# A decoder layer on one core: 48 weight units loaded ahead, gathers in steps 7 to 116 with a step's lag, the last 24 units in two rings of buffers

## The chip, the core and the metric

The kernel runs on one core of a Trainium2 chip, in one launch. The metric is device time in microseconds. Its engines: TensorE (PE, matmuls; PEld is its loading of weights), VectorE (DVE), ScalarE (ACT), GpSimd (POOL) and SyncE (SP, which here only starts transfers). Each engine works through its own list of instructions in order; a list is fixed when the program is built, and semaphores make an instruction wait for others.

## What is computed

A layer over 256 tokens of width 2048: a projection, a pooling mixer beside sparse attention, an output projection and a layer norm, then a retrieval among 128 x 128 = 16384 experts, and a second norm. The change lies in the retrieval:

```python
v1, i1 = lax.top_k(s1, PEER_TOPK)            # 16 of 128 keys, twice
v2, i2 = lax.top_k(s2, PEER_TOPK)
best, pos = lax.top_k(cand, PEER_TOPK)       # 16 of the 256 pairs, for each of 8 heads
expert = jnp.take_along_axis(cidx, pos, axis=-1)
act = jax.nn.gelu(jnp.einsum('td,thkd->thk', xc, u[expert]), approximate=False)
out = jnp.einsum('thk,thkd->td', gate * act, v[expert])
```

Each token needs the products of its row with 128 chosen rows of u.

## The kernel before

Instead of gathering whole rows of u, the kernel multiplies the first 1408 of the 2048 columns densely, for all 16384 experts, and gathers only the last 640 columns. This is the u stage, and the change lies in it and in the stage ahead of it.

**The dense part** runs over 128 steps (`i2`). A step is 11 pieces of 128 columns, each multiplied in three matmuls (`mm3`: high and low halves of float32). The weights come in units of 512 columns by 128 partitions, four pieces each: 352 units, 2.75 in a step. A unit is loaded by SP (256 KB), split into `hi` (ACT, L95) and `lo` (DVE, L96; in the first 20 units every fourth on POOL) and multiplied. There are four `hi`/`lo` pairs, so splits run at most four units ahead of PE. At the end of a step ACT copies the sums into `S` (L687).

**Where units wait.** `S` fills up step by step, and its parts that are not yet written serve as buffers: a planner (L520 to L532) gives unit n a place in `S`, and `load_ahead` (L534) loads it when unit m is split. `PRE` sets how many loads go out in the stage before, while the last 12 column tiles of the query projection `w_q` (48 units, in a ring of four `raw` buffers) are worked on. `PRE = (1, 2)` is one in two, thus 24. The last 24 units (`RAW_END`) find no place in `S` and pass through the four `raw` buffers.

**The gathered part** is 256 gathers, one for each slot and half of the tokens: POOL starts a transfer of 128 rows of 640 numbers (L666), and DVE multiplies it with the tokens' columns and sums (L691, called a product below). `spread` deals them out over the steps `G0` to `GE`, here 12 to 124, each gather and its product in one step. Their buffers are a ring of three (`gath`) and, two times in five (`GR = 2`), the ring of four `raw`, which the last 24 units share. Indices (`e_idx`) come from the top-16 search, head by head, mostly on DVE.

The order of each engine's list is set by a scheduler from program order and priorities; loads and splits of units have a high priority (`AHEAD`). After the u stage come the extraction (32 blocks of 8 tokens; `at`, `bt` and `a_hot` on DVE and POOL, loads `bc` in the ring `gath`, products `junk` L733) and the v stage, which is built like the u stage. The change leaves the lists of the v stage as they were, and those of the extraction but for its first blocks.

Of the kernel before, what the change touches and what calls it, by code (L numbers as in the profile page):

```python
# [9 lines left out]
F32 = mybir.dt.float32  # L10
# [8 lines left out]
P = 128  # L19
# [12 lines left out]
GU = D - KDU * P  # L32
# [6 lines left out]
UNIT = 512  # L39
EB = 8  # L40
GB = 3
GR = 2
GR_END = 128
RB = 4
RAW_END = 24
FIRST = 2
# [4 lines left out]
IDLE = 28  # L51
EARLY0 = 16
EARLY_N = 2
PRE = (1, 2)
BP = 3
AHEAD = 3000
G0 = 12
GE = 125
LEAD = 5
LAG = 1  # L60
KEEP0 = 40
# [11 lines left out]
def layer(ctx, tc, A, out):  # L73
    nc = tc.nc
# [10 lines left out]
    def bankA(name):  # L85
        return psA.tile([P, 512], F32, name=name, tag="a")
# [4 lines left out]
    last_split, last_copy, last_load, last_moment = [None], [None], [None], [None]  # L91
    after_unit = [None]

    def split(hi, lo, src, eng=None):
        last_copy[0] = nc.scalar.copy(hi, src).ins  # L95
        last_split[0] = (eng or nc.vector).tensor_tensor(lo, src, hi.bitcast(F32), op=ALU.subtract).ins  # L96

    def raw_unit():
        return stream.tile([P, UNIT], F32, name="raw", bufs=RB)

    def load_unit(src, raw=None, eng=None):
        with tc.high_priority(offset=AHEAD):
            if raw is None:
                raw = raw_unit()
                last_load[0] = nc.sync.dma_start(raw, src).ins
            pair = tuple(stream.tile([P, UNIT], F32R, name=s, bufs=4) for s in ("hi", "lo"))
            split(pair[0], pair[1], raw, eng)
        return pair
# [10 lines left out]
    def mm3(o, l, r, first, last):  # L119
        mm(o, l[0], r[0], start=first, stop=False)  # L120
        mm(o, l[0], r[1], start=False, stop=False)  # L121
        return mm(o, l[1], r[0], start=False, stop=last).ins  # L122
# [9 lines left out]
    gath = ctx.enter_context(tc.tile_pool(name="gath", bufs=1))  # L132
# [370 lines left out]
    def step_of(i2, sl=slice(0, T)):  # L503
        return S[:, i2 // 2, sl.start // 2:sl.stop // 2, i2 % 2, :]
# [4 lines left out]
    def s_part(p):  # L509
        return S[:, p].rearrange("p a b c -> p (a b c)")  # L510

    def paired(a):
        return a.rearrange("p (t j) -> p t j", j=2)
# [5 lines left out]
    U_UNITS = P * KDU // 4  # L519
    place, follow, free, n = {}, {}, set(range(1, P // 2)), 0  # L520
    for m in range(-WQ_UNITS, U_UNITS):
# [3 lines left out]
        n = max(n, m + 1)  # L525
        for _ in range((m * PRE[0] % PRE[1] < PRE[0]) if m < 0 else 2):
            fit = [p for p in free if 2 * p > (4 * n + 3) // KDU + 1]
# [6 lines left out]
    def load_ahead(m):  # L534
        for n in follow[m]:
            p = place[n]
            with tc.issue_after(last_load[0]):
                last_load[0] = nc.sync.dma_start(s_part(p), A["u_d"][n]).ins

    count = [-WQ_UNITS]  # L540
# [117 lines left out]
    gorder = [(tt, h * PK + k) for h in range(HEADS) for k in range(PK) for tt in range(NT)]  # L658

    def gather(table, tt, slot, n):  # L660
        if table is A["u_g"] and slot < GR_END and count[0] % (GB + GR) >= GB:
            g = stream.tile([P, n], F32, name="g", tag="raw", bufs=RB)
        else:
            g = gath.tile([P, n], F32, name="g", bufs=GB)
        count[0] += 1
        nc.gpsimd.indirect_dma_start(out=g, out_offset=None, in_=table,  # L666
                                     in_offset=bass.IndirectOffsetOnAxis(ap=e_idx[:, tt, slot:slot + 1], axis=0))
        return g

    def spread(i, i0, i1):  # L670
        n = i1 - i0
        return gorder[len(gorder) * min(max(i - i0, 0), n) // n:len(gorder) * min(max(i - i0 + 1, 0), n) // n]

    after_unit[0] = None
    count[0] = 0
    w = None
    for i2 in range(P):
        ps = bankA("ups")[:, :T]
        for kt in range(KDU):
            un, k = divmod(i2 * KDU + kt, 4)  # L680
            if k == 0:
                p = place.get(un)
                w = load_unit(A["u_d"][un], None if p is None else s_part(p),
                              nc.gpsimd if un < POOL_UE and un % 4 in POOL_UU else None)
                load_ahead(un)
            mm3(ps, tuple(a[:, k * P:(k + 1) * P] for a in w), hs[kt], kt == 0, kt == KDU - 1)
        nc.scalar.copy(step_of(i2), paired(ps))  # L687
        with tc.issue_after(last_split[0]):
            for tt, slot in spread(i2, G0, GE):
                g = gather(A["u_g"], tt, slot, GU)  # L690
                nc.vector.scalar_tensor_tensor(g, g, 1.0, h_gath[:, tt], op0=ALU.mult, op1=ALU.mult,  # L691
                                               accum_out=pd[:, tt, slot:slot + 1])

# [92 lines left out]
    for m in range(P * NC):  # L786
        v_follow[m] = []
        i2, c = divmod(m, NC)
# [9 lines left out]
    def v_unit(i2, c):  # L798

        m = i2 * NC + c  # L800
        for n in v_follow[m]:
            with tc.high_priority(offset=AHEAD), tc.issue_after(last_load[0]):
                last_load[0] = nc.sync.dma_start(s_part(v_place[n]), A["v_d"][n]).ins
        return s_part(v_place[m]) if m in v_place else None
# [38 lines left out]
    for i2 in range(P - GL):  # L843
        wt = weights(i2, tokens if i2 == 0 else [slice(0, T)])
        units = []
        for c in range(NC):
            raw = v_unit(i2, c)
# [113 lines left out]
```

## Time and profile before

| | us |
|---|---|
| three runs | 1741.22, 1744.06, 1749.92 (median 1744.06) |
| the profiled execution | 1744.31 |
| its span, from the first instruction to the last | 1742.5 |
| PE busy / DVE busy / ACT busy / POOL busy | 1667.0 / 1433.3 / 899.2 / 872.9 |
| u stage: copy of step 0 to copy of step 127 | 492.20 to 1006.72 |

The profile is of one execution; durations below come from it. An engine's busy time in a stretch is shown beside the stretch's length; "PEclk" is the granted clock of TensorE as a share of its full speed. A matmul's record is longer than the distance between two, since they are pipelined: it is the distance that counts.

### The profile page before, as it was taken

The page shows a single profiled execution, that of the slowest core. Times are in us where ns is not written, and L with a number is a line of the kernel's source. Part 1 is how long each engine was busy: PE and PEld are TensorE (multiplying, and loading weights), DVE is VectorE, ACT ScalarE, POOL GpSimd, SP SyncE. Part 2 cuts the span into 40 slices and gives each one's busy share as a digit, 9 for nine tenths or more (in the row PEclk, how much of TensorE's full clock was granted, in tenths as well). Part 3 has the DMA queues.
Part 4 walks back from the last instruction along what each step waited for, and adds up shares of the span by engine and source line. Part 5 has one row for each costly group of instructions (what it writes and reads, how often), then busy time and mean ns, then how long its engine had stood idle before and what let it go on. Part 6 is the DMA issues. An engine that isn't in the chain of part 4 may idle for free. (4 is left out here: it accounts for less than half of the span.)

```text
span 1742.5 us, 33159 instructions
## 1 busy us (share of the span) xinstructions
PE 1667.0 (96%) x10680; PEld 1487.2 (85%) x10680; DVE 1433.3 (82%) x3486; ACT 899.2 (52%) x1917; POOL 872.9 (50%) x892
## 2 busy tenths in 40 slices
PE   8999999999899999999999889988999999999996
PEld 8999888889889999999999788876787888888883
DVE  6766677679999989888888798876778888889896
ACT  6545565444445555555554357764454555555551
POOL 0000000026886666566665588857647644556562
PEclk9999999999999999999999999999999999999998
DMA  7667667826688999999999932138999999999962
GB/s 219 177 188 193 198 184 253 258 93 218 217 288 290 343 352 337 318 338 353 340 334 321 306 107 59 52 104 287 303 327 327 381 334 331 340 314 329 354 199 89
DMA packets 206014, 451.13 MB, mean 259 GB/s; under 512 B 26928, under 2 KB 31472, under 8 KB 205328
## 3 DMA queue, kind: packets, MB, share of 16 engines
q1 hardware_dynamic: 164816, 297.93, 52.4%
q0 software_dynamic: 41024, 151.09, 25.0%
q8 instruction: 84, 1.38, 0.3%
q14 instruction: 90, 0.74, 0.1%
HBM read 444.59 MB, written 4.26 MB: 258 GB/s over the span
## 5 line engine op out<-in xcount | busy, mean ns | idle before, releaser
L95 ACT CAST hi<-S 128x512 fp32r<-128x512 f32 x677 | 420.0, 621 | 430.2 <-PE vacc L122 220.0
L96 DVE TENSOR_TENSOR lo<-S,hi 128x512 fp32r<-128x512 f32 x672 | 463.0, 698 | 95.8 <-ACT hi L95 88.0
L122 PE MATMUL ups<-hTh,lo 128*128 128x256 f32 x1408 | 391.8, 282 | 8.2 <-DVE lo L96 8.1
L120 PE MATMUL ups<-hTh,hi 128*128 128x256 f32 x1408 | 393.2, 281 | 4.4 <-ACT hi L95 4.2
L121 PE MATMUL ups<-hTl,hi 128*128 128x256 f32 x1408 | 392.8, 280 | 0.0
L666 POOL DMA_INDIRECT g<-u_g,e_idx x256 | 286.3, 1118 | 172.3 <-DVE g L691 121.2
L95 ACT CAST hi<-raw 128x512 fp32r<-128x512 f32 x327 | 201.3, 620 | 209.4 <-PE projT L121 58.9
L96 DVE TENSOR_TENSOR lo<-raw,hi 128x512 fp32r<-128x512 f32 x303 | 215.7, 716 | 111.8 <-ACT hi L95 110.0
L121 PE MATMUL vacc<-lo,wt 128*128 128x512 f32 x744 | 278.7, 401 | 6.9 <-DVE lo L96 6.8
L122 PE MATMUL vacc<-hi,wt 128*128 128x512 f32 x744 | 275.9, 398 | 0.0
L122 PEld LDWEIGHTS ups<-hTh,lo 128*128 128x128 f32 x1408 | 263.7, 189 | 13.0 <-DVE lo L96 12.1
L120 PEld LDWEIGHTS ups<-hTh,hi 128*128 128x128 f32 x1408 | 266.1, 189 | 5.9 <-ACT hi L95 5.9
L121 PEld LDWEIGHTS ups<-hTl,hi 128*128 128x128 f32 x1408 | 266.1, 189 | 0.0
L120 PE MATMUL vacc<-hi,wt 128*128 128x512 f32 x744 | 232.4, 401 | 7.5 <-ACT wt L95 6.9
L812 POOL DMA_INDIRECT g<-v_g,e_idx x139 | 161.7, 1163 | 130.7 <-DVE accg L820 107.6
L691 DVE SCALAR_TENSOR_TENSOR g<-g,h_gath 128x640 f32<-128x640 f32 x256 | 205.1, 821 | 14.7 <-DMA g<-u_g,e_idx 14.4
L812 POOL DMA_INDIRECT raw<-v_g,e_idx x117 | 138.0, 1179 | 85.3 <-DVE accg L820 67.0
L121 PEld LDWEIGHTS vacc<-lo,wt 128*128 128x128 f32 x744 | 141.2, 190 | 43.9 <-DVE lo L96 9.2
L120 PEld LDWEIGHTS vacc<-hi,wt 128*128 128x128 f32 x744 | 141.6, 191 | 42.9 <-ACT wt L95 7.5
L122 PEld LDWEIGHTS vacc<-hi,wt 128*128 128x128 f32 x744 | 141.2, 190 | 33.9 <-issue 0.5
L721 POOL TENSOR_SCALAR bt<-cst,slotT 128x128 f32<-128x128 f32 x192 | 125.5, 671 | 27.3 <-POOL bt L721 15.9
L295 POOL TENSOR_TENSOR bias<-bias,score 128x128 f32<-128x128 f32 (+1 forms) x16 | 11.3, 731 | 234.1 <-DMA bias<-relb 110.9
(241 smaller groups left out, 3067.4 us busy)
## 6 DMA issues: line engine op xcount, KB each, us to landing
S<-v_d SPq DMA_DIRECT2D x361, 256.0 KB, 5.1
S<-u_d SPq DMA_DIRECT2D x328, 256.0 KB, 5.4
raw<-w_t SPq DMA_DIRECT2D x100, 256.0 KB, 2.9
raw<-w_n SPq DMA_DIRECT2D x64, 256.0 KB, 2.9
raw<-w_o SPq DMA_DIRECT2D x64, 256.0 KB, 3.5
raw<-w_q SPq DMA_DIRECT2D x48, 256.0 KB, 3.2
bc<-i_dram SPq DMA_DIRECT2D x32, 256.0 KB, 3.3
raw<-u_d SPq DMA_DIRECT2D x24, 256.0 KB, 4.9
```

Of the source, the lines that this page charges most:

```text
L95: last_copy[0] = nc.scalar.copy(hi, src).ins
L96: last_split[0] = (eng or nc.vector).tensor_tensor(lo, src, hi.bitcast(F32), op=ALU.subtract).ins
L120: mm(o, l[0], r[0], start=first, stop=False)
L121: mm(o, l[0], r[1], start=False, stop=False)
L122: return mm(o, l[1], r[0], start=False, stop=last).ins
L295: nc.gpsimd.tensor_tensor(bias[:, tt, :n], bias[:, tt, :n], sel[:, tt, :n], op=ALU.add)
L666: nc.gpsimd.indirect_dma_start(out=g, out_offset=None, in_=table, in_offset=bass.IndirectOffsetOnAxis(ap=e_idx[:, tt, slot:slot + 1], axis=0))
L691: nc.vector.scalar_tensor_tensor(g, g, 1.0, h_gath[:, tt], op0=ALU.mult, op1=ALU.mult, accum_out=pd[:, tt, slot:slot + 1])
L721: eng.tensor_scalar(bt[j][:, i], iota, i2T[:, t:t + 1], None, op0=ALU.is_equal)
L812: nc.gpsimd.indirect_dma_start(out=g, out_offset=None, in_=A["v_g"], in_offset=bass.IndirectOffsetOnAxis(ap=e_idx[:, tt, slot:slot + 1], a ...
```

## The change

Five edits, all in or ahead of the u stage:

- `PRE` becomes (1, 1): 48 loads of u units, not 24, go out among the 48 loads of `w_q`.
- Gathers are dealt out over steps 7 to 116 (110 steps) rather than 12 to 124 (113 steps).
- A gather's product comes one step after the gather (`fetched`, `due`).
- Until slot 116 gathers use the `raw` ring four times in seven, so both rings whole; the last 24 gathers two times in five.
- The last 24 units pass through both rings, three of seven through `gath` and four through `raw`.

```diff
-GR = 2
-GR_END = 128
+GR = (4, 2)
+GR_END = 116
-PRE = (1, 2)
+PRE = (1, 1)
-G0 = 12
-GE = 125
+G0 = 7
+GE = 117
...
-        if table is A["u_g"] and slot < GR_END and count[0] % (GB + GR) >= GB:
+        if count[0] % (GB + GR[slot >= GR_END]) >= GB:
...
-                w = load_unit(A["u_d"][un], None if p is None else s_part(p),
+                raw = None if p is None else s_part(p)
+                if un >= U_UNITS - RAW_END and un % (GB + RB) < GB:
+                    raw = gath.tile([P, UNIT], F32, name="g", bufs=GB)
+                    with tc.high_priority(offset=AHEAD):
+                        last_load[0] = nc.sync.dma_start(raw, A["u_d"][un]).ins
+                w = load_unit(A["u_d"][un], raw,
...
-            for tt, slot in spread(i2, G0, GE):
-                g = gather(A["u_g"], tt, slot, GU)
+            due, fetched = fetched, [(tt, slot, gather(A["u_g"], tt, slot, GU)) for tt, slot in spread(i2, G0, GE)]
+            for tt, slot, g in due:
```

What this does to the engines' lists, at three places. First DVE where the units change from `S` to the raw buffers (units 327 to 332), before. A row `lo<-S` or `lo<-raw` is the split of one unit, a row `g,pd<-g,h_gath` one product; the numbers tell tiles apart and grow in program order:

```order
L96 TENSOR_TENSOR lo_13140<-S_4968,hi_13139 128x512
L96 TENSOR_TENSOR lo_13166<-raw_13163,hi_13165 128x512
L96 TENSOR_TENSOR lo_13184<-raw_13181,hi_13183 128x512
L691 SCALAR_TENSOR_TENSOR g_13203,pd_6643<-g_13203,h_gath_75 128x640
L691 SCALAR_TENSOR_TENSOR g_12764,pd_6643<-g_12764,h_gath_75 128x640
L96 TENSOR_TENSOR lo_13210<-raw_13207,hi_13209 128x512
L691 SCALAR_TENSOR_TENSOR g_12815,pd_6643<-g_12815,h_gath_75 128x640
L691 SCALAR_TENSOR_TENSOR g_12818,pd_6643<-g_12818,h_gath_75 128x640
L96 TENSOR_TENSOR lo_13228<-raw_13225,hi_13227 128x512
L96 TENSOR_TENSOR lo_13246<-raw_13243,hi_13245 128x512
```

And the same place now, from the split of unit 327, over unit 328, to the last product of all, behind which stands the split of unit 329 (`lo_13226`):

```order
L96 TENSOR_TENSOR lo_13188<-S_4968,hi_13187 128x512
L697 SCALAR_TENSOR_TENSOR g_12981,pd_6667<-g_12981,h_gath_75 128x640
L697 SCALAR_TENSOR_TENSOR g_12763,pd_6667<-g_12763,h_gath_75 128x640
...
L697 SCALAR_TENSOR_TENSOR g_13090,pd_6667<-g_13090,h_gath_75 128x640
L96 TENSOR_TENSOR lo_13208<-raw_13205,hi_13207 128x512
L697 SCALAR_TENSOR_TENSOR g_12924,pd_6667<-g_12924,h_gath_75 128x640
L697 SCALAR_TENSOR_TENSOR g_12926,pd_6667<-g_12926,h_gath_75 128x640
L697 SCALAR_TENSOR_TENSOR g_12983,pd_6667<-g_12983,h_gath_75 128x640
L697 SCALAR_TENSOR_TENSOR g_13033,pd_6667<-g_13033,h_gath_75 128x640
L697 SCALAR_TENSOR_TENSOR g_13035,pd_6667<-g_13035,h_gath_75 128x640
L697 SCALAR_TENSOR_TENSOR g_13092,pd_6667<-g_13092,h_gath_75 128x640
L704 CAST iota_e_13659<-cst_295 128x256
L96 TENSOR_TENSOR lo_13226<-g_13223,hi_13225 128x512
```

Before, 231 products stand ahead of the split of unit 327 and the other 25 among those of units 328 to 351. Now 222 stand ahead of unit 312's split (before 215), 244 ahead of unit 327's, six between units 327 and 328, six between 328 and 329, and none behind.

Second, the end of POOL's gathers in the changed kernel, in the order in which they are started:

```order
L666 DMA g_12763<-u_g,e_idx_72 128x640
L666 DMA g_12811<-u_g,e_idx_72 128x640
L666 DMA g_12870<-u_g,e_idx_72 128x640
L666 DMA g_13088<-u_g,e_idx_72 128x640
L666 DMA g_13090<-u_g,e_idx_72 128x640
L666 DMA g_12924<-u_g,e_idx_72 128x640
L666 DMA g_12926<-u_g,e_idx_72 128x640
L666 DMA g_12983<-u_g,e_idx_72 128x640
L666 DMA g_13033<-u_g,e_idx_72 128x640
L666 DMA g_13035<-u_g,e_idx_72 128x640
L666 DMA g_13092<-u_g,e_idx_72 128x640
```

Of these, 13088 and 13090 lie in the `raw` ring; the other nine follow each other through the three buffers of `gath`, and the next three tiles in that ring are the units 329 to 331.

Third, where the products begin on DVE, behind the last indices. Before:

```order
L627 CAST i1b_6608<-i12_74 128x256
L96 TENSOR_TENSOR lo_7358<-S_4968,hi_7357 128x512
L691 SCALAR_TENSOR_TENSOR g_7313,pd_6643<-g_7313,h_gath_75 128x640
L691 SCALAR_TENSOR_TENSOR g_7316,pd_6643<-g_7316,h_gath_75 128x640
L691 SCALAR_TENSOR_TENSOR g_7368,pd_6643<-g_7368,h_gath_75 128x640
L691 SCALAR_TENSOR_TENSOR g_7371,pd_6643<-g_7371,h_gath_75 128x640
L96 TENSOR_TENSOR lo_7382<-S_4968,hi_7381 128x512
```

And now:

```order
L627 CAST i1b_6632<-i12_74 128x256
L96 TENSOR_TENSOR lo_7384<-S_4968,hi_7383 128x512
L697 SCALAR_TENSOR_TENSOR g_7063,pd_6667<-g_7063,h_gath_75 128x640
L697 SCALAR_TENSOR_TENSOR g_7065,pd_6667<-g_7065,h_gath_75 128x640
L697 SCALAR_TENSOR_TENSOR g_7117,pd_6667<-g_7117,h_gath_75 128x640
L697 SCALAR_TENSOR_TENSOR g_7119,pd_6667<-g_7119,h_gath_75 128x640
L697 SCALAR_TENSOR_TENSOR g_7173,pd_6667<-g_7173,h_gath_75 128x640
L697 SCALAR_TENSOR_TENSOR g_7175,pd_6667<-g_7175,h_gath_75 128x640
L697 SCALAR_TENSOR_TENSOR g_7229,pd_6667<-g_7229,h_gath_75 128x640
L96 TENSOR_TENSOR lo_7411<-S_4968,hi_7410 128x512
```

The products begin at the same place of the list, some 35 units in, with seven in a row where four stood; by unit 56 there are 22 where there were 18.

## Rows read from the trace of the kernel before

**Rows 1.** Stretches of the span: length, busy us of each engine, clock, transfers.
```profile
395.00:475.00 80.00, 74.28 (x603) 72.34 (x602) 75.13 (x301) 31.39 (x73) 62.94 (x72) 0.98 0.70 221
475.00:550.00 75.00, 70.35 (x573) 67.44 (x571) 71.96 (x241) 36.79 (x84) 55.30 (x65) 1.00 0.87 285
550.00:575.00 25.00, 24.33 (x205) 23.92 (x205) 23.02 (x50) 12.11 (x24) 17.12 (x17) 1.00 0.90 298
575.00:947.70 372.70, 372.43 (x3193) 372.23 (x3192) 326.52 (x679) 193.92 (x361) 231.59 (x206) 1.00 0.96 341
947.70:1006.70 59.00, 50.01 (x363) 46.36 (x361) 44.76 (x99) 21.23 (x41) 32.39 (x32) 0.94 0.89 291
```

**Rows 2.** Timeline of ACT, copies of steps 16, 116 and 127: start, duration.
```profile
562.02 0.39 ACT L687 COPY S<-ups 128x256 f32<-128x256 f32 x1
...
947.66 0.39 ACT L687 COPY S<-ups 128x256 f32<-128x256 f32 x1 [2.67 <-PE ups L122]
...
1006.72 0.40 ACT L687 COPY S<-ups 128x256 f32<-128x256 f32 x1 [1.99 <-PE ups L122]
```

**Rows 3.** Waits from 947.7 to 1006.7: who for whom, total, times, longest.
```profile
ACT hi L95 <- DMA raw<-u_d: 18.8, 12, 3.6
POOL g L666 <- DVE g L691: 16.7, 11, 3.5
...
DVE g L691 <- DMA g<-u_g,e_idx: 7.3, 8, 1.9
```

**Rows 4.** Timeline of DVE, two splits and the products behind them.
```profile
948.59 1.29 DVE L96 TENSOR_TENSOR lo<-S,hi 128x512 fp32r<-128x512 f32 x2 [2.04 <-ACT hi L95]
949.80 0.82 DVE L691 SCALAR_TENSOR_TENSOR g<-g,h_gath 128x640 f32<-128x640 f32 x1
...
952.04 0.82 DVE L691 SCALAR_TENSOR_TENSOR g<-g,h_gath 128x640 f32<-128x640 f32 x1
...
952.78 0.69 DVE L96 TENSOR_TENSOR lo<-S,hi 128x512 fp32r<-128x512 f32 x1
```

**Rows 5.** Gathers (L666), 947.7 to 1006.7: starts, and time from start to landing.
```profile
L666 POOL DMA_INDIRECT g<-u_g,e_idx x25: 942/1082/1384, 950.9 to 994.7; - x25
...
DMA to landing us min/median/max: 4.0/5.5/6.7
```

**Rows 6.** Raw loads (L105), the same stretch.
```profile
L105 SPq DMA_DIRECT2D raw<-u_d x22: 327/328/1147, 951.4 to 998.6; - x22
...
DMA to landing us min/median/max: 2.7/4.9/6.4
```

**Rows 7.** Two stretches of the tail, columns as in rows 1.
```profile
938.00:978.00 40.00, 35.34 (x283) 33.46 (x282) 31.40 (x68) 15.58 (x30) 22.51 (x21) 1.00 0.92 310
978.00:982.00 4.00, 4.00 (x22) 3.89 (x22) 3.22 (x8) 1.63 (x3) 1.89 (x3) 0.57 0.87 282
```

**Rows 8.** Waits from 395 to 475, the query projection.
```profile
ACT hi L95 <- DMA raw<-w_q: 14.3, 14, 3.2
...
PE wq L122 <- DVE lo L96: 4.6, 4, 1.6
```

**Rows 9.** Timeline of DVE around the start of the extraction.
```profile
1004.50 0.69 DVE L96 TENSOR_TENSOR lo<-raw,hi 128x512 fp32r<-128x512 f32 x1 [1.19 <-ACT hi L95]
...
1008.38 1.37 DVE L723 TENSOR_TENSOR a_hot<-iota_e,i1Tb 128x1024 bf16<-128x1024 bf16 x2
...
1010.85 0.28 DVE L733 SCALAR_TENSOR_TENSOR junk<-eps,bt 128x128 bf16<-128x128 f32 x1
```

**Rows 10.** The page's transfers: source line, count, KB, median us to landing.
```profile
S<-u_d SPq DMA_DIRECT2D x328, 256.0 KB, 5.4
...
raw<-w_q SPq DMA_DIRECT2D x48, 256.0 KB, 3.2
bc<-i_dram SPq DMA_DIRECT2D x32, 256.0 KB, 3.3
```

**Rows 11.** The page's costliest groups: ACT's split, and its idle time before.
```profile
L95 ACT CAST hi<-raw 128x512 fp32r<-128x512 f32 x327 | 201.3, 620 | 209.4 <-PE projT L121 58.9
```

More of the change, by code (lines that the diff above doesn't have):

```diff
@@ L675, in layer @@
     count[0] = 0
-    w = None
+    w, fetched = None, []
     for i2 in range(P):
```

## The prediction

> **What bounds the kernel now.** I read the stretches first, then the copies at the ends of steps, then waits, and last how long single instructions and transfers take. From 575 to 947.7 PE is busy 372.43 of 372.70 us at the full clock (2.4 GHz): matmuls bound the middle of the u stage, with DVE at 88% and the transfers at 96% of their engines' time right behind [rows 1]. The copies of steps 16 and 116 lie 385.64 us apart, thus 3.856 us a step, and a step is 2.75 units: 1.402 us of PE for a unit [rows 2]. From the copy of step 116 to that of step 127 it takes 59.06 us where 11 steps at that pace are 42.4: the tail loses 16.6 us [rows 2]. What is waited for there: ACT 18.8 us for raw loads of the last units, POOL 16.7 us for buffers that DVE frees, DVE 7.3 us for gathers [rows 3]. Four raw buffers serve 24 loads and the last gathers at once. Ahead of the u stage it is DVE that is full: 75.13 of 80 us, then 71.96 of 75 and 23.02 of 25, and PE loses 5.7, 4.7 and 0.7 us [rows 1]. So the change can take back at most those 16.6 us in the tail, and it touches a stretch at the start where DVE has no room.
>
> **Loads ahead.** 24 more loads go out among those of w_q; the bytes are the same, only earlier. No wait for a load into S shows among the waits of the first steps, so there is nothing to gain: cost between 0 and, if each of 24 loads holds up a w_q load by its own length (262 KB at the 341 GB/s of rows 1, 0.77 us), 18 us on ACT. ACT already waits 14.3 us for w_q loads, yet PE's wait there is for DVE [rows 8], which hides most: I take 1 us. Nor is the stock larger when the gathers begin: by the planner the load of unit 88 goes out at unit 32 before and at unit 37 now, since S is full in either case.
>
> **Gathers from step 7.** The product list on DVE still begins behind the last indices, at the same unit. What changes is the density: 22 products by unit 56, not 18. A product takes (952.04 - 949.80)/3 = 0.747 us, a split (949.80 - 948.59)/2 = 0.61 [rows 4]. Four more are 3.0 us, on an engine with 2 us left in 25. Cover is at most the four pairs of splits; without it 3.0, and with gathers landing late up to 4.5 (six products); low end 0. I take 2.5.
>
> **The middle.** 222 products by unit 312 against 215, so 7 more in some 256 units beyond the four, on an engine with 46 us of idle time [rows 1]: nothing, PE still bounds. The lag of a step frees nothing here either, because what a gather waits for is its buffer.
>
> **The tail.** This is the term that decides. It removes the sharing of raw buffers: after unit 329 there is no gather left, seven buffers serve a load that lands in 4.9 us [rows 6] and 1.402 us of PE each, so units 329 to 351 cost no stall; 16.6 us go. But all 256 products now stand ahead of the split of unit 329, and PE cannot pass that split.
>
> First DVE alone. From the split of unit 312 to that of unit 329 stand 34 products and 17 splits: 25.4 + 10.4 = 35.8 us. PE has at most four units in hand, less the 1.3 us that a new split takes (0.62 on ACT [rows 11], 0.69 on DVE [rows 4]), 4.3 us, and 16 units to do, 22.4: 26.7 us. It would wait 9.1 us even if every gather lay ready. That is the floor.
>
> Then the chain of buffers. Up to the split of unit 327, DVE has 22 products and 15 splits, 25.6 us, against 21.0 of PE: the 4.3 us in hand are spent. After that split come two products (1.5 us), the second of which frees a gath buffer; the gather that waits for it lands 5.5 us later [rows 5] and is multiplied (0.75); the next the same; then the load of unit 329 takes the buffer, 4.9 us [rows 6], and is split (1.3). The sum is 1.5 + 12.5 + 6.2 = 20.2 us, hand-overs between engines left out, in which PE has units 327 and 328, 2.8 us. It waits 17.4 us. By the shortest landings of rows 5 and 6 (4.0 and 2.7) and with 4.3 us still in hand it is 9.3; by the longest (6.7 and 6.4) 21.3. A stop costs clock too: after the gaps up to 978, four microseconds run at 0.57 of the full clock, near the 1.2 GHz level, with 22 matmuls where 34 fit [rows 7], 1.4 us. And products wait for landings ahead of the chain: 7.3 us in 25 products of the tail before [rows 3, 5], for 22 products 6.4, of which I take half, 3.2, since there are more buffers. Together 17.4 + 1.4 + 3.2 = 22.0, from 9.1 to 26; against 16.6 that is +5.4, from -7.5 to +9.4.
>
> The Trainium skill (SBUF — State Buffer, The DMA setup-cost knee) gives a transfer about 2 us plus its bytes at 436 GB/s; as an estimate that is 2.75 us for a gather and 2.6 for a load, and the chain would be 12.4 us, PE's wait 9.6 and the forecast some 8 us less. The trace does not agree under this load, as rows 5 and 6 measured 5.5 and 4.9, so the sum goes by them.
>
> **Start of the extraction.** The split of unit 351 can now end 4.3 us ahead of PE's end, where it was 1.5 (1005.2 to 1006.7 [rows 2, 9]). That would give 2.8 us, but the loads bc pass through gath behind the units, and the third is issued only after that split and lands 3.3 us later [rows 10]; six at, six bt and two a_hot follow before the first product, which before took from 1005.2 to 1010.85 with their like [rows 9]. It comes out about 4.8 us after PE's end where it was 4.1: +1, between -2.8 and +2.
>
> **Sum.** The profiled execution took 1744.31 us (span 1742.5), 0.25 above the median of the runs, so no correction. 1744.3 + 1.0 + 2.5 + 0 + 5.4 + 1.0 = 1754.2: 1754 us.
>
> **Rivals.**
>
> A, faster: the chain stays covered. Place: the split of unit 329; price: its wait is DVE's floor of 9.1 us or the chain's lower end of 9.3, and DVE's hand at the start suffices. It decides if gathers land in 4 us once the loads into S end, and if the pairs are still full at unit 327. For it: POOL's shortest landing is 4.0 [rows 5], and 22 products may have been ready early with seven buffers. Against it: DVE's count of 25.6 against 21.0 empties the hand whatever lands when. 1744.3 - 7.0 + 1 = 1738 us. The knee rule above points this way.
>
> B, no change: the wait changes its owner. The chain costs what the shared buffers cost, 16 to 19 us, and the denser start is half hidden. For it: both tails are the same bytes through the same engines, and the middle is bound by PE in both. Time: 1744 to 1751, say 1748.
>
> C, slower by more: loads of S in front of each w_q load. PE lost 5.7 us there while ACT waited 14.3 [rows 1, 8]; the 18 us of added delay passed on at that ratio (0.4) are 7.4, so 1754.2 - 1 + 7.4 = 1761. Against it: w_q loads land in 3.2 us [rows 10] in a ring that turns in four times 80/48 = 6.7 us.
>
> D: the change does not do what it says. In part this is seen already: the first product does not move. If the early gathers only sat in their buffers, the denser start would be free, 1754.2 - 2.5 = 1752; I count it with the forecast.
>
> **How the numbers follow.** Forecast 0.50, A 0.16, B 0.21, C 0.13. About 0.5% (8.7 us) is what a measurement of this kernel can tell from no change: faster is below 1735.3, slower above 1752.8. The forecast's own spread is about 1748 to 1761, 0.8 of it above that bound; C is above it nearly whole; B is within; A lies on both sides of the lower bound. Slower 0.40 + 0.12 = 0.52, faster 0.09, same 0.39. The range takes in most of A's upper half and C: low 1739, high 1765; the likeliest case alone has 1748 to 1761.
>
> **What would show it.** In the changed profile the copies between steps 16 and 116 keep 3.856 us; one gap of PE of 8 to 18 us stands before the first matmul of unit 329 (step 119), with a smaller one at unit 328, and DVE waits for gathers in it; from there to the last copy about 33 us without a gap, ACT no longer waiting for raw loads. The copy of step 127 comes some 9 us later than 1006.7. The granted clock falls once behind the gap. Between 475 and 600 PE loses 2 to 3 us more, named as a wait for DVE's lo. I am wrong if PE's gap at unit 329 is under 9 us, if the tail's loss is spread over many steps, or if the w_q stage grows by more than 3 us.

## The result and the profile after

The changed kernel took 1752.54 us (median of 15 runs, 1748.93 to 1759.21), the kernel before 1741.71 beside it: a ratio of 1.0061, 95% interval 1.0048 to 1.0075, 10.8 us slower by the medians. The forecast was 1754, slower. The profiled execution of the changed kernel took 1749.17 us (span 1747.4), 3.4 below its median, and that of before 1744.31, 2.6 above the median of before; so the two traces show 4.9 us of the 10.8, and each term is read at its own place.

Stretches of the changed kernel's span (length, then busy us of PE, PEld, DVE, ACT, POOL, then granted clock, transfers' share, GB/s; they answer to [rows 1, 7]):

```profile
395.00:475.00 80.00, 75.03 (x608) 72.97 (x607) 74.58 (x300) 32.08 (x74) 62.69 (x73) 0.98 0.87 290
475.00:550.00 75.00, 69.74 (x561) 66.44 (x559) 71.21 (x244) 36.44 (x81) 55.67 (x65) 1.00 0.63 199
550.00:575.00 25.00, 21.85 (x177) 21.04 (x178) 21.97 (x50) 10.22 (x19) 19.03 (x19) 1.00 0.97 345
575.00:930.70 355.70, 355.70 (x3051) 355.70 (x3050) 314.50 (x652) 185.43 (x344) 224.68 (x200) 1.00 0.96 342
953.60:965.00 11.40, 8.23 (x67) 7.82 (x66) 9.81 (x24) 2.44 (x6) 8.33 (x8) 1.00 0.95 323
965.00:983.60 18.60, 8.40 (x38) 6.89 (x37) 11.30 (x28) 4.14 (x8) 6.01 (x6) 0.64 0.82 260
983.60:1014.30 30.70, 30.68 (x262) 30.47 (x261) 15.88 (x26) 13.96 (x27) 4.11 (x7) 1.00 0.68 195
```

The middle is bound by PE in both kernels. The new hole is the sixth row: in 18.6 us PE works 8.4. Behind it PE runs through to the end of the u stage.

The copies of steps 0, 20, 111, 118, 119 and 127 in ACT's timeline (start, duration), which answer to [rows 2]:

```profile
491.13 0.38 ACT L693 COPY S<-ups 128x256 f32<-128x256 f32 x1
...
581.00 0.39 ACT L693 COPY S<-ups 128x256 f32<-128x256 f32 x1
...
930.71 0.39 ACT L693 COPY S<-ups 128x256 f32<-128x256 f32 x1 [2.32 <-PE ups L122]
...
965.08 0.39 ACT L693 COPY S<-ups 128x256 f32<-128x256 f32 x1 [4.20 <-PE ups L122]
983.65 0.39 ACT L693 COPY S<-ups 128x256 f32<-128x256 f32 x1
...
1014.32 0.39 ACT L693 COPY S<-ups 128x256 f32<-128x256 f32 x1 [3.46 <-PE ups L122]
```

In the kernel before the same six stand at 492.20, 577.93, 928.59, 957.04, 962.16 and 1006.72. Step 0 is 1.1 us earlier; from there to step 20 it takes 89.87 us instead of 85.73 (+4.1); from step 111 to 127, where 16 steps at 3.856 would be 61.7, it takes 83.61 instead of 78.13. Below, "tail loss" is that time less 61.7: 16.4 before, 21.9 after. Steps 118 and 119 alone are 26.15 us where 7.7 would do.

What is waited for from 947.7 to 1013 (total, times, longest), against [rows 3]:

```profile
ACT hi L95 <- DMA g<-u_d: 12.3, 2, 11.5
...
DVE g L697 <- DMA g<-u_g,e_idx: 7.2, 9, 1.4
...
PE slotTp L646 <- DVE g L697: 6.6, 2, 5.4
```

Of ACT's 18.8 us for raw loads 1.7 are left; one wait of 11.5 us for the gath load of unit 329 has come. DVE around it, from the split of unit 327 to that of unit 329:

```profile
962.84 0.68 DVE L96 TENSOR_TENSOR lo<-S,hi 128x512 fp32r<-128x512 f32 x1
963.45 0.81 DVE L697 SCALAR_TENSOR_TENSOR g<-g,h_gath 128x640 f32<-128x640 f32 x1
...
969.19 0.69 DVE L96 TENSOR_TENSOR lo<-raw,hi 128x512 fp32r<-128x512 f32 x1
969.80 0.82 DVE L697 SCALAR_TENSOR_TENSOR g<-g,h_gath 128x640 f32<-128x640 f32 x1
...
972.02 0.83 DVE L697 SCALAR_TENSOR_TENSOR g<-g,h_gath 128x640 f32<-128x640 f32 x1 [1.40 <-DMA g<-u_g,e_idx]
...
975.30 0.83 DVE L697 SCALAR_TENSOR_TENSOR g<-g,h_gath 128x640 f32<-128x640 f32 x1 [1.30 <-DMA g<-u_g,e_idx]
...
978.52 0.82 DVE L697 SCALAR_TENSOR_TENSOR g<-g,h_gath 128x640 f32<-128x640 f32 x1 [0.84 <-DMA g<-u_g,e_idx]
...
979.90 0.69 DVE L96 TENSOR_TENSOR lo<-g,hi 128x512 fp32r<-128x512 f32 x1 [0.22 <-PE slotTp L646]
```

From the end of unit 327's split (963.5) to the end of unit 329's (980.6) it takes 17.1 us, in which PE has some two units to do. PE in the same stretch:

```profile
958.44 0.39 PE L120 MATMUL ups<-hTh,hi 128*128 128x256 f32 x1 [0.51 <-ACT hi L95]
...
961.60 0.38 PE L122 MATMUL ups<-hTh,lo 128*128 128x256 f32 x1 [2.66 <-DVE lo L96]
...
967.80 0.39 PE L120 MATMUL ups<-hTh,hi 128*128 128x256 f32 x1 [1.93 <-ACT hi L95]
...
969.93 0.48 PE L122 MATMUL ups<-hTh,lo 128*128 128x256 f32 x1 [1.63 <-DVE lo L96]
...
971.92 0.41 PE L122 MATMUL ups<-hTh,lo 128*128 128x256 f32 x1
977.74 0.48 PE L646 MATMUL slotTp<-cst,pd 128*128 128x128 f32 x1 [5.40 <-DVE g L697]
979.41 0.47 PE L646 MATMUL slotTp<-cst,pd 128*128 128x128 f32 x1 [1.20 <-DVE g L697]
979.92 0.58 PE L120 MATMUL ups<-hTh,hi 128*128 128x256 f32 x1
```

It waits at unit 325 first (958.44 to 961.60), before the chain begins, then at unit 328 (967.80 to 969.93), and last ahead of unit 329 (979.92). In that last place stands something that the prediction did not name: the transposes of `pd` (slotTp, L646), which need the last product, come ahead of unit 329's matmuls.

### The profile page after: what moved, and what is told of

Read it like the earlier page. It is cut to its first block, busy times and chain, and to the rows that moved or that the text cites. A ratio compares the mean times of both kernels' runs of the same rounds, so it can differ in the third digit from the quotient of the medians.

```text
span 1747.4 us, 33152 instructions
## 1 busy us (share of the span) xinstructions
PE 1660.8 (95%) x10680; PEld 1480.1 (85%) x10680; DVE 1431.5 (82%) x3486; ACT 899.6 (51%) x1917; POOL 869.4 (50%) x892
## 5 line engine op out<-in xcount | busy, mean ns | idle before, releaser
L666 POOL DMA_INDIRECT g<-u_g,e_idx x256 | 284.4, 1111 | 153.3 <-DVE g L697 98.0
L96 DVE TENSOR_TENSOR lo<-raw,hi 128x512 fp32r<-128x512 f32 x292 | 208.3, 716 | 113.9 <-ACT hi L95 112.5
L95 ACT CAST hi<-raw 128x512 fp32r<-128x512 f32 x316 | 195.1, 620 | 201.2 <-PE projT L121 53.0
L122 PEld LDWEIGHTS ups<-hTh,lo 128*128 128x128 f32 x1408 | 263.5, 189 | 18.4 <-DVE lo L96 17.0
L826 DVE SCALAR_TENSOR_TENSOR accg<-g,pd,accg 128x512 f32<-128x512 f32 x139 | 109.6, 791 | 25.1 <-DMA g<-v_g,e_idx 24.7
```

Source lines behind the costliest of these rows:

```text
L826: nc.vector.scalar_tensor_tensor(accg[:, tt], g, pd[:, tt, slot:slot + 1], accg[:, tt], op0=ALU.mult, op1=ALU.add)
```

## Experiments

All times are medians beside runs of the kernel before on the same chip. Runs e1 to e4 were on a chip where before takes 1741.15 us; e5 to e8 on another (1751.65) and e9 to e12 on a third (1751.00), where the u stage takes longer. So e9 runs the changed kernel again, for e10 to e12 to stand beside. In the profiles of e5 to e12 many landings are not recorded (e9 has 20,166, the changed kernel's first profile 26,539), and some waits there are named "issue" or "remote", which means that the profile knows no instruction that ended them.

**e1, loads ahead alone** (before, edited):

```
-PRE = (1, 2)
+PRE = (1, 1)
```

> The kernel before, with only the load-ahead changed: 48 units of u go out among the loads of w_q, not 24. Theory: the loads among those of w_q cost nothing, since PE waits for DVE there; the copy of step 0 came 1.1 us earlier in the changed kernel's profile, not later. Expected -1 to +1 us against before (about 1742), tail loss 16 us as before. Rival (a load into S delays each w_q load and the delay is passed on at 0.4): +7 us, 1749.

1743.06 against 1741.15, ratio 1.0003 [0.9986, 1.0020]; step 0's copy at 491.43, tail loss 16.1. No cost and no gain of the loads among those of w_q is clear of the noise of 3 us, and the rival of +7 us is out.

**e2, first gathers from step 12** (changed kernel, edited):

```
-G0 = 7
+G0 = 12
```

> The changed kernel, with the first gathers spread from step 12 again, all else as changed. Theory: the denser start of the products costs the 3 to 4 us that the copies of steps 0 and 20 lay further apart (89.87 us against 85.73), and the middle, bound by PE, does not give it back; the tail is unchanged. Expected 3 us less than the changed kernel, about 1749, +7 against before, tail loss 22 us. Rival (the start is paid back elsewhere, for instance because more products in the steps up to 116 cost the same time there): the time of the changed kernel, 1752 to 1753.

1748.82, ratio 1.0036 [1.0022, 1.0051], where the change has 1.0061. From step 0 to 20 it takes 84.24 us, 5.6 less than in the change; the tail was to stay at 22 and loses 24.9, 3.0 more. The medians give the start about 4 us of the 10.8, though the two intervals just meet; the steps from 20 to 105 take 326.8 us as in the change (326.6), and give none of it back.

**e3, ring turned by four** (changed kernel, edited):

```
-if un >= U_UNITS - RAW_END and un % (GB + RB) < GB:
+if un >= U_UNITS - RAW_END and (un + 4) % (GB + RB) < GB:
```

> The changed kernel, with the ring of the last 24 units turned by four: units 328 to 331 come through raw buffers, 332 to 334 through gath buffers. Theory: the large gap stands where the first unit takes a gath buffer from the gathers, so it moves from unit 329 to unit 332 (step 120) and shrinks, as three more units (4.2 us of PE) can run while the last gathers pass; 2 to 5 us less than the changed kernel, 1748 to 1751. Rival (the time of DVE for the last products is the cause, whatever buffer a unit has): the loss of the tail stays 20 to 24 us and the time 1752 to 1753.

1747.81, ratio 1.0041 [1.0025, 1.0057]; tail loss 21.0. A gap moved to step 120, as expected (972.10 to 984.91 between the copies of 119 and 120, 9.0 us more than a step needs), while steps 118 and 119 still lose 8.9. But it is not held there by a gath load:

```profile
980.91 0.37 ACT L647 COPY slotT<-slotTp 128x256 f32<-128x256 f32 x1 [8.43 <-PE slotTp L646]
981.18 1.14 ACT L95 CAST hi<-g 128x512 fp32r<-128x512 f32 x2
```

That is ACT's timeline: the copy of `pd`'s transpose stands ahead of unit 332 and waits for the last product; the unit's load, issued at 976.7, landed 3.5 us later, some 0.7 us before that copy. So the chain through the gath buffer and the last product end almost together, and this run can't tell them apart. The place is the theory's; the tail loss, 21.0, is the rival's, and the gain in time is not clear of the noise, as the interval overlaps that of the change. What the theory left out: in the lists of the change and of e3 the last product closes PE and ACT too, for what stands behind `pd`'s transposes in their queues.

**e4, before's spread with two rings** (changed kernel, edited):

```
-G0 = 7, GE = 117
+G0 = 12, GE = 125
```

> The changed kernel, with before's spread of gathers (steps 12 to 124): the last 24 units still pass through raw and gather buffers in turn, now with gathers between them. Theory: what costs the tail its 22 us is that all products stand ahead of the split of unit 329; spread to step 124, a unit's split stands behind at most three products, DVE's work for the last 40 units (some 24 us of splits and 30 of products) fits into 56 us of PE, and seven buffers are shared. Expected tail loss 3 to 10 us and start as before: 1730 to 1738, faster than both. Rival (buffers shared by gathers and units cost what they cost before, 16 us): 1742 to 1746.

1754.76, ratio 1.0075 [1.0053, 1.0097], some 17 us above the theory's upper end. The tail loses 33.5 us. Its waits from 940 to 1020:

```profile
POOL g L666 <- DVE lo L96: 29.7, 7, 15.5
ACT hi L95 <- DMA g<-u_d: 21.7, 9, 3.7
...
ACT hi L95 <- DMA raw<-u_d: 12.2, 5, 6.0
```

Gathers now wait for splits of units, and unit loads for products, in both rings: POOL stands 15.5 us before one gather. DVE had room, as expected: it is busy 44.6 of the 80 us. Two rings without the early end lose more in the tail than the change (33.5 against 21.9); that they take longer in all is not shown, as the intervals overlap.

**e5, early end alone** (before, edited):

```
-GE = 125
+GE = 117
```

> The kernel before, with one number changed: gathers are spread over steps 12 to 116, not 12 to 124; one ring of raw buffers for the last units, no lag, 24 units loaded ahead. Theory: the 16 us that the tail of before loses come from raw buffers shared by 24 loads and the last gathers; with gathers over eight steps earlier most of the loads have the raw buffers alone, and no unit needs a gath buffer that the last gathers hold. Tail loss 6 to 11 us, time 1733 to 1737. Rival (the denser products ahead of the last splits are what costs the changed kernel its tail, whatever ring the units use): tail loss 18 to 22, 1743 to 1748.

1771.68 against 1751.65, ratio 1.0101 [1.0078, 1.0123], in spite of the smallest tail loss of all, 5.1 us, and the last copy 512.37 us behind step 0's (before 514.52). The loss is in the next stage: the first junk product comes 25.4 us behind the last copy, not 4.1. POOL's timeline there:

```profile
1001.40 1.16 POOL L666 DMA_INDIRECT g<-u_g,e_idx  x1 [0.69 <-DVE g L691]
1002.60 10.64 POOL L721 TENSOR_SCALAR bt<-cst,slotT 128x128 f32<-128x128 f32 x15
1013.40 1.05 POOL L666 DMA_INDIRECT g<-u_g,e_idx  x1 [0.17 <-issue]
...
1025.09 0.95 POOL L666 DMA_INDIRECT g<-u_g,e_idx  x1 [0.30 <-issue]
```

The new lists put the last products behind all splits, and 24 one-hot tiles of the extraction ahead of the last gathers on POOL; bc, which passes through the same gath buffers, goes out at 1022.6 only. The tail loss came out under the theory's 6 to 11; the time was to fall by 5 to 9 us and rose by 20. Since products left the tail for the stage behind it, the run does not show that the buffers were what the tail lost by.

**e6 and e11, one ring** (changed kernel, with the five lines that load units into gath buffers taken out).

> The changed kernel, with all of the last 24 units in raw buffers (no unit passes through a gath buffer); loads ahead, steps 7 to 116, lag and the pattern of the gathers' buffers as in it. Theory: the gap of 16 us at unit 329 is a chain through gath buffers (product, gather, product, load, split), so it goes with the gath loads; left are the denser start (+3 to 4) and what DVE's bunched products cost: tail loss 11 to 16, 1743 to 1747. Rival (DVE's time for all products ahead of unit 329): tail loss 20 to 22, 1750 to 1753.

> The kernel of e6 (all of the last 24 units in raw buffers) beside the changed kernel on the same chip. Theory (the chain ends in a gath buffer that a unit needs): no gap at unit 329, tail loss 5 to 9 us below the changed kernel's, time 3 to 8 us below it. Rival (DVE's time): both as the changed kernel.

1765.70 (ratio 1.0074 [1.0050, 1.0098]) and 1765.24 (1.0086 [1.0069, 1.0103]). On the chip of e11, e9 takes 1770.23: 5 us more. Tail loss 19.3 and 19.0; e9 has 28.2. The tail of e6 was to lose 11 to 16. No single gap stands at unit 329; steps 118 and 119 are 13.1 us in e11 and 25.7 in e9. So the gap comes from the units' way through gath buffers and from what the lists make of it: in e11 the last products stand between the splits of raw units, and PE meets `pd`'s transposes at 1000.6 us without a wait.

**e7, last gathers over all seven buffers** (changed kernel, edited):

```
-GR = (4, 2)
+GR = (4, 4)
```

> The changed kernel, with the last gathers too spread over all seven buffers (three gath, four raw; the changed kernel gives gathers from step 116's slots on only two raw buffers of every five). Theory (chain of buffers): with more buffers the last gathers go out a landing sooner and the gath buffer of unit 329 is freed 3 to 5 us sooner, though now unit 328 waits for a raw buffer too: 1748 to 1751, the gap still in front of units 328 and 329. Rival (DVE's time): same products ahead of the same split, time as the changed kernel, 1752 to 1753.

1768.53, ratio 1.0096 [1.0077, 1.0115], tail loss 22.7. e9 (1.0119 [1.0097, 1.0141], 28.2) came from another chip and the intervals meet, so the gain of a landing is likely and not shown.

**e9, the changed kernel again** (no edit).

> The changed kernel itself, beside the next three on one chip, since in the last four runs instructions came late on ACT, DVE and PE, which no profile of before or of the changed kernel shows; so those four have nothing to stand beside. Theory: +9 to +12 us against before where instructions come in time, tail loss 22; where they come late as in the last runs, +14 to +20.

1770.23, ratio 1.0119 [1.0097, 1.0141]: 19 us. Step 0 to 20 takes 96.6 us, the tail loses 28.2.

**e8 and e10, short products** (changed kernel, edited; products from step 108 on leave out 624 of 640 columns):

```
+n = 16 if i2 >= 108 else GU
 nc.vector.scalar_tensor_tensor(g[:, :n], g[:, :n], 1.0, h_gath[:, tt, :n], ...)
```

> The changed kernel, but products issued from step 108 on multiply only the first 16 of 640 columns (the rest of these products is left out); every gather is still made in full, and the list of DVE is the same. A product then takes some 0.1 to 0.2 us, not 0.747. Theory (chain of buffers): the gathers and the load behind the split of unit 327 still land one after the other, two landings of 5 us, a load of 3 to 5 and 1.3 us of splitting, 14 to 17 us against 2.8 of PE and up to 4.3 in hand: the gap at units 328 and 329 stays at 7 to 12 us and the tail loses 8 to 14. Rival (DVE's time is what costs): tail loss under 5 us.

> The kernel of e8 (from step 108 on products multiply 16 of 640 columns, the rest of these products is left out) beside the changed kernel on the same chip. Theory (chain of buffers and landings): the gap at units 328 and 329 stays, and the loss of the tail is 2 to 8 us below the changed kernel's. Rival (DVE's time for 34 products and 17 splits is the cause): the loss of the tail falls by 15 us or more, to under 7.

1771.86 (1.0121 [1.0096, 1.0146]) and 1773.58 (1.0134 [1.0113, 1.0155]): no faster than e9 at 1.0119. Tail loss 28.7 and 29.2. The rival, which had the tail loss under 5 or 7 us, is out; the theory's fall of 2 to 8 us did not come either. Two stretches of e10, the first ahead of the gap, the second in it, columns as above:

```profile
970.00:980.00 10.00, 2.85 (x17) 2.01 (x16) 0.73 (x8) 0.40 (x1) 7.26 (x8) 0.84 0.92 323
985.00:1003.00 18.00, 10.16 (x55) 8.74 (x54) 3.89 (x17) 3.46 (x8) 5.52 (x6) 0.69 0.77 239
```

The same of e9, the second at 984 to 1002:

```profile
970.00:980.00 10.00, 7.10 (x49) 6.67 (x49) 7.06 (x18) 2.32 (x5) 7.78 (x8) 0.84 0.94 332
984.00:1002.00 18.00, 7.38 (x39) 6.17 (x39) 8.60 (x21) 3.47 (x8) 4.75 (x5) 0.69 0.70 213
```

DVE is almost empty in e10 (0.73 of 10 us, 3.89 of 18), and PE waits all the same. Its timeline of DVE from the split of unit 327 on:

```profile
983.71 0.69 DVE L96 TENSOR_TENSOR lo<-S,hi 128x512 fp32r<-128x512 f32 x1
984.31 0.17 DVE L698 SCALAR_TENSOR_TENSOR g<-g,h_gath 128x16 f32<-128x16 f32 x1
...
990.52 0.17 DVE L698 SCALAR_TENSOR_TENSOR g<-g,h_gath 128x16 f32<-128x16 f32 x1 [0.56 <-DMA g<-u_g,e_idx]
...
995.04 0.17 DVE L698 SCALAR_TENSOR_TENSOR g<-g,h_gath 128x16 f32<-128x16 f32 x1 [2.28 <-DMA g<-u_g,e_idx]
...
998.57 0.17 DVE L698 SCALAR_TENSOR_TENSOR g<-g,h_gath 128x16 f32<-128x16 f32 x1 [1.66 <-DMA g<-u_g,e_idx]
...
999.85 0.69 DVE L96 TENSOR_TENSOR lo<-g,hi 128x512 fp32r<-128x512 f32 x1 [0.77 <-ACT hi L95]
```

The chain from split to split is 16.1 us (984.4 to 1000.5), 18.7 in e9 (980.4 to 999.1): four products in a row, each 0.58 us shorter, explain 2.3 of the 2.6. Most of what is left is waits for landings. What was saved came back ahead of it: the copies of steps 116 and 117 are 10.1 us apart in e10, 6.2 in e9 and 3.9 in the changed kernel's first profile. ACT in e10:

```profile
981.48 0.38 ACT L693 COPY S<-ups 128x256 f32<-128x256 f32 x1 [9.67 <-remote]
981.76 1.65 ACT L95 CAST hi<-S 128x512 fp32r<-128x512 f32 x3
```

The first row is the copy of step 117. By PE's records the sums of that step were done at 972.1; the copy waits for PE's signal alone, and the signal that released it is recorded at 981.46, over 9 us later. The last three loads into S did not hold it: the landings of them that are recorded lie between 968.4 and 971.5, DVE's own wait for the load of unit 325 is over at 975.3, and ACT splits all three without a wait behind the copy. What held the signal, and with it ACT's splits and PE, stays open. e11 has a stop there too (7.8 us between the copies). So e10 and e9 differ by more than the length of the products, and the pair shows what the products do to the chain better than what they do to the time.

**e12, a version from what was seen** (changed kernel, edited; the gath loads of units taken out as in e6):

```
-GR = (4, 2), GR_END = 116, G0 = 7
+GR = (4, 1), GR_END = 112, G0 = 12
```

> What the runs so far point to: start at step 12, end at 117 with the lag, 48 units ahead, the last 24 units in raw buffers alone, and gathers of slots from 112 on in three gath buffers and one raw buffer of every four gathers, so that raw buffers pass to the units early; the products stay spread between the splits to the end, and none is left for the stretch after the last copy, where e5 lost its 21 us behind POOL's one-hot tiles. Theory: start as before (no 3 to 4 us), tail loss 8 to 12 us, extraction 4 us after the last copy: 4 to 8 us below before. Rival (gathers through few buffers come late, and products hold up splits or POOL's tiles as in e4 and e5): at or above before, +0 to +12.

1749.93 against 1751.00, ratio 1.0005 [0.9989, 1.0021]: the time of before, and 20 us below the changed kernel on that chip. Step 0 to 20 takes 85.9 us, the tail loses 12.7, the extraction starts 5.4 us behind the last copy. The theory's 4 to 8 us below before did not come; the time is at the rival's lower end. No version tried here beats the kernel before.

## Why the prediction was right, and where it was not

Time, sign and the place of the loss were right, and so was the chain as a mechanism. The close numbers are in part luck: in the tail three wrong sizes cancel, and the forecast's base, 1744.3, lay 2.6 us above the median that before showed beside the change. Of the prediction's own signs of being wrong one came: PE's gap at unit 329 was to be 9 us or more, and it is 8.0 from the last matmul of unit 328 (971.92) to the first of unit 329 (979.92); the rest of the wait stands at units 325 and 328. Term by term:

- **Loads ahead, +1.0:** -1.1 at step 0 in the trace, 1.0003 in e1; nothing clear of noise, and rival C is out. ACT waits 16.1 us for w_q loads against 14.3 [rows 8], and PE's wait for DVE there fell from 4.6 to 3.9.
- **Denser start, +2.5:** a term that was mis-sized. It measured +4.1 in the trace, near the upper end of 4.5, and about 4 by the medians of e2 (5.6 between its first copies). I had let the pairs of splits cover some of the products; PE's waits for DVE's lo from 475 to 575 went from 3.3 to 7.0 us.
- **Middle, 0:** from step 20 to 105 it takes 326.6 us, before 327.3. Nothing.
- **Tail, 22.0 lost:** 21.9 from step 111 on: steps 112 to 117 lose 3.6, steps 118 and 119 lose 18.4, and the last eight nothing. The total was met by luck. By the distances between PE's matmuls some 3.5 of the 18.4 us stand at unit 325, ahead of the chain; some 12 stand in the chain, where the sum had 17.4; the rest, some 3, is the low clock, where it had 1.4. So 7.1 us are lost ahead of the chain, for which the sum had 3.2. The clock was granted at 0.64 from 965.0 to 983.6, and at 1.00 behind it. In the 60.7 us from step 116 itself, the stretch that the prediction used, 18.3 are lost, since part of it lies ahead of step 116. The chain was 17.1 us long, not 20.2: the gathers issued behind the split of unit 327 landed in 4.3 us in the median (3.6 to 5.1; 5.5 in the sum), and the load of unit 329 took 3.1 (issued 976.20, split by ACT at 979.25), near the lower end of [rows 6].
- **DVE ahead of the chain:** the count of 25.6 us held. From the split of unit 312 to that of unit 327 (935.5 to 963.5) DVE is busy 25.2 of 27.9 us, where PE needs 21.0; 1.6 of the rest are waits for gathers. PE's hand was spent, as said, and its wait at unit 325 is for these splits. That DVE's 9.1 us would stay as a floor, with every gather ready, was not tested. With DVE nearly idle e10 loses as much, but on another chip and with a stop that the first profile doesn't have, so it does not settle what DVE alone costs.
- **What closes PE:** I named the split of unit 329. The transposes of `pd` close it too, and in e3 they do it some 0.7 us after the unit's load has landed.
- **Extraction, +1:** the first junk product comes 4.48 us behind the last copy, before 4.13: +0.35.

With 0.3 us gained from step 105 to 111 these sum to -1.1 + 4.1 - 0.7 - 0.3 + 5.5 + 0.35, about 7.9, and the first junk product is 7.95 us later (1018.80, before 1010.85 [rows 9]). Behind it the profiled execution won 3 us back in stages whose lists are the same. From the first junk product to the last accumulating one, before, the change and e1 to e4 took 699.8, 696.8, 695.4, 700.6, 698.7 and 697.1 us, so this is the spread of one execution; the medians of 15 runs show 10.8.

Rival A (a covered chain) needed landings of 4 us, and with 4.3 it nearly had them; what it lacked was its other condition, full pairs at unit 327, as PE had waited for DVE at unit 325 already. Rival B (the wait changes its owner) is half of what happened: the tail lost 21.9 us where B had 16 to 19, and the start was not hidden. By the rule in the Trainium skill (SBUF — State Buffer, The DMA setup-cost knee) the chain would be 12.4 us, as an estimate, and the trace says 17.1: its gathers took 4.3 us in the median against 2.75, and only the load of unit 329, issued behind the last gather, comes near the rule with 3.1 us against 2.6.

## What to carry to other kernels

Work taken out of a shared ring moves the wait to whatever the freed work now stands behind: before ending a stream of gathers earlier, find the last product in every engine's list (DVE's splits, PE's transposes, ACT's copy, POOL's next stage), for each of them holds all that follows. A chain that alternates transfers and short operations is priced by the landings measured where it will stand (here 4.3 us, not the 5.5 of the whole tail before); making the operations shorter took 2.6 of 18.7 us off the chain, and no gain in time was measured. A sum that comes out right must still be checked term by term, as errors can cancel. Measure to the end of the kernel and not of the stage: e5 had the best u stage and one of the worst times.

## What the runs showed of the hardware that I had not expected

The chip counts. The same changed kernel costs 1.0061 [1.0048, 1.0075] beside before where before takes 1742 us, and 1.0119 [1.0097, 1.0141] where it takes 1751. The stretch from 575 to 700, in the changed kernel's first profile and in e9:

```profile
575.00:700.00 125.00, 125.00 (x1074) 125.00 (x1073) 112.25 (x234) 65.67 (x122) 81.35 (x73) 1.00 0.96 348
```

```profile
575.00:700.00 125.00, 123.57 (x1047) 122.82 (x1047) 106.50 (x227) 62.30 (x117) 75.21 (x70) 1.00 0.91 318
```

The transfers move 318 GB/s instead of 348, while PE has already lost 6.7 us more by step 20 (96.6 against 89.9). From 700 to 900 both move about 340. Whether the transfers are slower on those chips, or only start later, these profiles can't tell; nor do they say what delays the copy of step 117 there. A profile of before from such a chip was not taken. It matters for reading: a kernel whose loss lies in waits for transfers should be compared on one chip.
